# Moving weight splits of the second gate pair, the second up pair and the last gate matrix from POOL to DVE in a fused streaming-encoder block

## The chip, the cores and the metric

The kernel runs on one core of one Trainium2 chip. The metric is the device time of one execution in microseconds (us). Five queues of instructions run beside each other and meet at semaphores: TensorE (PE, with its weight loads as PEld), VectorE (DVE, `V` in the code), ScalarE (ACT, `A`), GpSimd (POOL, `G`) and SyncE (SP), which issues most transfers. Each engine takes its instructions strictly in the order of its queue.

## The reference

One layer over 1024 positions of 1024 features, all in float32. Cut to what matters here:

```python
u = rmsnorm(h, g_mix_pre);  z = u @ w_in            # ... gate_a, gate_b are two of its pieces
mixed = sigmoid(gate_a) * ya + sigmoid(gate_b) * yb # ya: conv mixer, yb: latent attention
h = h + rmsnorm(mixed @ w_o, g_mix_post)
u2 = rmsnorm(h, g_ffn_pre)
up = causal_dwconv3(u2 @ w_ffn_up) + b              # 2 x 2816 columns
f = (gelu(up[:, :2816]) * up[:, 2816:]) @ w_ffn_down
h = h + rmsnorm(f, g_ffn_post)
e = p @ w_ple_proj
g = sigmoid(h @ w_ple_gate)
return h + rmsnorm(e * g, g_ple_post)
```

## The kernel before, in words

**Three products for one.** Each operand of a matmul is held as a high part `hi` (the value cast to fp32r, L182, always on ACT) and a low part `lo` (value minus `hi`, L183, on the engine that the caller names). A product is hi·hi + lo·hi + hi·lo. `split` makes the two parts; `block` splits 512 columns, `wide` 1024 columns at once.

**Pairs.** The large products (`w_in`'s gates, `w_up`, `w_down`) are done by a scheme of seven instead of eight block products. For two 128-column blocks of weights, `weights` loads two 128x1024 tiles and forms combinations: it splits A22, adds A21 to A22 in place (L337), subtracts to make S3 (L338), then makes S1 (here L339), S2's and S4's tile (L340) and splits both tiles with `wide`. Its argument `who` names the engine for the split of A11/A12, for the split of A22, for L337 and for L338; L339, L340 and the last two splits are always DVE's. `pair` then runs the block products (`prod`, L307) into PSUM banks taken from a ring, and adds them up from PSUM on DVE (L367, L368, L377 to L383). An "early" pair has its first row done beforehand by `first_row`, and runs five products; its first sum, L366, is POOL's. The activations have the same kind of combinations (T1 to T4), made once a stage by `x_blocks`; `third` splits T3, T1 and T4.

**Three stages matter here.** In the gate stage (from about 70 us), pairs 2 to 5 of `w_in` come first; the first one's weights are made by DVE alone (`(V, V, V, V)`), those of the others by `(V, G, G, G)`. In the up stage (from about 815 us) the pairs follow `order`; again the first one's weights are DVE's, those of the rest are POOL's in the same four places. In the end stage (from about 1350 us) come the last products of the down projection (`down_tail`, L217, added up at L964), the norm of the second half of the features (`second_residual`, whose scaled rows are L1048, residual sums L1049 and splits the operand `hX`), then the gate product of the per-layer embedding with its own norm. `square_sum` squares on ACT (L250) and adds on DVE (L253).

**What sets the order.** The order within each queue is set when the kernel is built, by a scheduler that simulates the program; `tc.issue_after(x)` tells it only to place what is inside behind `x`, and adds no wait on the chip. Waits come from data, from PSUM banks and from the buffers ("slots", `s`) that are used again. `raws` is a ring of buffers for raw weights, `wblk` one of seven buffers for split weights.

Of the kernel before, what the change touches and what calls it, by code (L numbers as in the profile page):

```python
# [77 lines left out]
def kernel(  # L78
# [53 lines left out]
    def f32r(i):  # L132
        return slot(i, F32R)
# [7 lines left out]
    def singles(*slots):  # L141

        return [(i, h) for i in slots for h in range(2)]
# [5 lines left out]
    def f(ap):  # L149
        return ap.bitcast(F32)  # L150
# [39 lines left out]
        split(src, hi[:, :n], lo[:, :n], eng or G)  # L190
        return hi, lo

    def wide(src, eng):

        hi, lo = f32r(wblk()), f32r(wblk())
        split(src, hi, lo, eng)
        return [(hi[:, hs(i)], lo[:, hs(i)]) for i in range(2)]

    def load_w(src, raws, cols=1024, dst=(None, None), eng=None):

        raw = f32(raws())
        nc.sync.dma_start(raw[:, :cols], src)
        return [block(raw[:, c : min(c + HALF, cols)], eng, d) for c, d in zip(range(0, cols, HALF), dst)]

    def load_all(w, raws, others):

        where = [None] * NBLK + list(others)
        return [load_w(w[c], raws, dst=where[2 * c : 2 * c + 2]) for c in range(8)]

    def linear(out_ps, w, wc, X, half, cs=None, start=True, stop=True):  # L210

# [115 lines left out]
    def weights(src0, src1, raws, early=False, who=(V, G, G, G)):  # L327

        r0, r1 = f32(raws()), f32(raws())
        nc.sync.dma_start(r1, src1)  # L330
        nc.sync.dma_start(r0, src0)
        a11, a12, a21, a22 = r0[:, hs(0)], r0[:, hs(1)], r1[:, hs(0)], r1[:, hs(1)]
        w = {}
        if not early:
            w["A11"], w["A12"] = wide(r0, who[0])
        w["A22"] = block(a22, who[1])
        who[2].tensor_add(a22, a21, a22)  # L337
        w["S3 made"] = who[3].tensor_sub(a21, a11, a21)  # L338
        V.tensor_sub(a11, a22, a11)  # L339
        V.tensor_sub(a12, a12, a11)  # L340
        w["S2"], w["S4"] = wide(r0, V)
        w["S3"], w["S1"] = wide(r1, V)
        w["end"] = last[-1]
        return w
# [107 lines left out]
    def gate_weights(i, early=False, who=(V, G, G, G)):  # L452
        return weights(w_in[17 + 2 * i], w_in[18 + 2 * i], raws, early, who)
# [23 lines left out]
    for n, i in enumerate(range(2, 6)):  # L477
        if n:
            with tc.issue_after(behind):
                w = gate_weights(i, True)  # L480
        gate_pair(i, early[n], others(), True, w=w)
    for i in range(2):
        spilled_pair(i, early[i])
# [421 lines left out]
    mm = Ring(range(4))  # L905

    def up_weights(j):
        return weights(w_up[j], w_up[NFF + j], raws, j in rows, (G, G, G, G) if j != order[0] else (V, V, V, V))

    w = up_weights(order[0])  # L910
    behind = third(w)
# [119 lines left out]


    hrs = Ring(singles(12, 9))
    sqs, sqs2, accs = Ring(singles(extra[2])), Ring(singles(extra[3])), Ring(singles(50))
    hX = [[None, None] for _ in range(8)]
    hslots = [*range(29, 33), *range(13, 17)], range(17, 25)
    SS, RB = 6, 7

    def second_residual(h):
        acc = None  # L1040
        for k in range(8):
            acc = square_sum(acc, single(yacc[k], h), accs, sqs)
        R = rstd(acc, D, SS, RB)
        for k in range(8):
            hr = single(*hrs())
            nc.sync.dma_start(hr, d_h1[k, :, hs(h)])
            y = single(yacc[k], h)
            V.scalar_tensor_tensor(y, y, col("g_ffn_post", k), R, op0=ALU.mult, op1=ALU.mult)  # L1048
            (G if k % 2 else V).tensor_add(hr, hr, y)  # L1049
            hX[k][h] = parts(hslots[h][k])  # L1050
            split(hr, *hX[k][h], V if k % 2 else G)

    second_residual(0)
    down_tail(fX, 1)
    second_residual(1)

    mm = Ring(range(4))
    sbk, rbk = Ring([4, 5, 6]), Ring([7])
    ers, ors = Ring(singles(10, 11)), Ring(singles(42, 12, 9, 7, 8))
    wgs = load_all(w_gate, raws, [*range(25, 29), 43, *range(38, 42)])  # L1060
    for h, o, n in ((0, 0, 512), (1, 0, 256), (1, 256, 256)):
        acc = None
        cs = slice(o, o + n)
        base = h * HALF + o
        for ft in range(8):
            er = single(*ers())[:, :n]
            nc.sync.dma_start(er, d_e[ft, :, base : base + n])
            pt = bank(mm())[:, :n]
            linear(pt, wgs[ft], 0, hX, h, cs)
            g_ = single(yacc[ft], h)[:, cs]  # L1070
            A.activation(g_, pt, AF.Sigmoid)
            V.tensor_mul(g_, g_, er)  # L1072
            acc = square_sum(acc, g_, accs, sqs2)
        R = rstd(acc, D, sbk(), rbk(), n)
        for k in range(8):
            o_ = single(*ors())[:, :n]
            g_ = single(yacc[k], h)[:, cs]
            hi, lo = hX[k][h]
            G.tensor_add(o_, f(hi[:, cs]), f(lo[:, cs]))
            V.scalar_tensor_tensor(g_, g_, col("g_ple_post", k), R, op0=ALU.mult, op1=ALU.mult)  # L1080
            (G if k in (0, 2, 4) else V).tensor_add(o_, o_, g_)  # L1081
            (nc.sync if k % 2 else A).dma_start(out[k * P : (k + 1) * P, base : base + n], o_)
# [101 lines left out]
```

## Time and profile before

| | us |
|---|---|
| runs | 1517.89, 1518.36, 1521.10 |
| median | 1518.36 |
| profiled execution | 1521.76 |
| its span, first to last instruction | 1520.0 |

| engine | busy us | share of span | instructions |
|---|---|---|---|
| PE | 1472.8 | 97% | 6980 |
| PEld | 1227.8 | 81% | 6980 |
| DVE | 1180.4 | 78% | 1654 |
| ACT | 700.8 | 46% | 1100 |
| POOL | 522.7 | 34% | 383 |

PE works 97% of the span, so it stands for 47 us; the mean granted clock of this execution is 0.989 of full speed. The busy shares of the other engines are means over stages that differ much, and are read by stage below. All rows further down come from the profiled execution.

### The profile page before, as it was taken

The page shows a single profiled execution, that of the slowest core. Times are in us where ns is not written, and L with a number is a line of the kernel's source. Part 1 is how long each engine was busy: PE and PEld are TensorE (multiplying, and loading weights), DVE is VectorE, ACT ScalarE, POOL GpSimd, SP SyncE. Part 2 cuts the span into 40 slices and gives each one's busy share as a digit, 9 for nine tenths or more (in the row PEclk, how much of TensorE's full clock was granted, in tenths as well). Part 3 has the DMA queues.
Part 4 walks back from the last instruction along what each step waited for, and adds up shares of the span by engine and source line. Part 5 has one row for each costly group of instructions (what it writes and reads, how often), then busy time and mean ns, then how long its engine had stood idle before and what let it go on. Part 6 is the DMA issues. An engine that isn't in the chain of part 4 may idle for free. (4 is left out here: it accounts for less than half of the span.)

```text
span 1520.0 us, 19261 instructions
## 1 busy us (share of the span) xinstructions
PE 1472.8 (97%) x6980; PEld 1227.8 (81%) x6980; DVE 1180.4 (78%) x1654; ACT 700.8 (46%) x1100; POOL 522.7 (34%) x383
## 2 busy tenths in 40 slices
PE   8999999999989999999999999999999999999896
PEld 6878888888778888788887788888888888787796
DVE  6897666567558888753668889999998889978786
ACT  8634322336447777343454444444434634334333
POOL 1245122236533433341124243344331021333953
PEclk9999999999999999999999999999999999999898
DMA  9444322345841012542381223333335542433432
GB/s 343 158 140 157 122 78 59 114 171 187 272 165 48 20 56 88 190 140 63 118 300 45 97 89 119 125 125 114 114 120 175 183 168 70 125 118 111 140 105 96
DMA packets 74368, 198.72 MB, mean 131 GB/s; under 512 B 7456, under 2 KB 22304, under 8 KB 74272
## 3 DMA queue, kind: packets, MB, share of 16 engines
q1 hardware_dynamic: 65920, 173.04, 35.0%
q10 hardware_dynamic: 8352, 24.44, 4.2%
q8 instruction: 55, 0.90, 0.3%
q14 instruction: 41, 0.34, 0.1%
HBM read 144.89 MB, written 52.56 MB: 130 GB/s over the span
## 5 line engine op out<-in xcount | busy, mean ns | idle before, releaser
L307 PE MATMUL psum<-s,s 128*128 128x512 f32 x3948 | 906.5, 391 | 10.5 <-DVE s L367 5.2
L307 PEld LDWEIGHTS psum<-s,s 128*128 128x128 f32 x3948 | 742.7, 189 | 168.9 <-DVE s L367 5.6
L182 ACT CAST s<-s 128x1024 fp32r<-128x1024 f32 (+3 forms) x419 | 336.8, 828 | 400.6 <-PE psum L307 128.9
L217 PE MATMUL psum<-s,s 128*128 128x512 f32 (+1 forms) x1920 | 417.2, 375 | 17.3 <-ACT s L182 11.2
L183 POOL TENSOR_TENSOR s<-s,s 128x512 fp32r<-128x512 f32 (+2 forms) x147 | 219.9, 1508 | 558.5 <-PE psum L307 337.2
L217 PEld LDWEIGHTS psum<-s,s 128*128 128x128 f32 x1920 | 337.3, 192 | 81.3 <-ACT s L182 13.0
L183 DVE TENSOR_TENSOR s<-s,s 128x1024 fp32r<-128x1024 f32 (+2 forms) x272 | 325.3, 1215 | 65.0 <-ACT s L182 51.8
L543 DVE SCALAR_TENSOR_TENSOR psum<-s,vecs,psum 128x1023 f32<-128x1023 f32 (+1 forms) x88 | 111.7, 1278 | 4.3 <-ACT psum L541 3.3
L541 ACT ACTIVATE psum<-s,vecs 128x1024 f32<-128x1024 f32 x44 | 53.1, 1208 | 88.5 <-DVE s L379 74.3
L183 DVE TENSOR_TENSOR s<-psum,s 128x512 fp32r<-128x512 f32 (+3 forms) x144 | 70.8, 504 | 29.0 <-ACT s L182 27.9
L366 POOL TENSOR_TENSOR s<-s 128x512 f32<-128x512 f32 x24 | 45.8, 1908 | 135.5 <-DVE s L323 80.5
L182 ACT CAST s<-psum 128x512 fp32r<-128x512 f32 (+3 forms) x144 | 61.1, 445 | 41.8 <-DVE s L183 12.7
L250 ACT ACTIVATE s<-s 128x512 f32<-128x512 f32 (+1 forms) x68 | 38.9, 580 | 72.0 <-DVE s L1072 29.5
L762 PE MATMUL psum<-s,s 128*128 128x512 f32 (+2 forms) x288 | 67.4, 359 | 2.3 <-ACT s L773 2.2
L775 POOL TENSOR_SCALAR s<-s,ri 128x384 f32<-128x384 f32 (+5 forms) x48 | 41.3, 860 | 70.3 <-DVE ri L774 55.5
L253 DVE TENSOR_TENSOR s<-s,s 128x512 f32<-128x512 f32 (+1 forms) x55 | 46.3, 842 | 15.3 <-ACT s L250 13.6
L787 PE MATMUL psum<-s,s 128*128 128x256 f32 x320 | 54.1, 292 | 1.5 <-DVE s L183 0.7
L762 PEld LDWEIGHTS psum<-s,s 128*128 128x128 f32 x288 | 46.4, 189 | 9.9 <-ACT s L773 5.3
L773 ACT ACTIVATE s<-psum,nm 128x128 f32<-128x128 f32 (+3 forms) x64 | 47.5, 745 | 14.3 <-DVE nm L771 9.0
L338 POOL TENSOR_TENSOR s<-s,s 128x512 f32<-128x512 f32 x37 | 52.8, 1428 | 2.9
L337 POOL TENSOR_TENSOR s<-s 128x512 f32<-128x512 f32 x37 | 51.0, 1378 | 2.9
L253 DVE TENSOR_TENSOR s<-s,psum 128x512 f32<-128x512 f32 x28 | 19.1, 685 | 41.1 <-ACT psum L250 40.4
(120 smaller groups left out, 1180.4 us busy)
## 6 DMA issues: line engine op xcount, KB each, us to landing
s<-in_w_up_dram SPq DMA_DIRECT2D x56, 512.0 KB, 3.7
s<-in_w_in_dram SPq DMA_DIRECT2D x42, 512.0 KB, 3.9
s<-in_w_down_dram SPq DMA_DIRECT2D x36, 512.0 KB, 3.7
d_f<-s SPq DMA_DIRECT2D x22, 512.0 KB, 2.6
s<-in_x_dram SPq DMA_DIRECT2D x32, 256.0 KB, 5.4
d_sg<-s ACTq DMA_DIRECT2D x16, 512.0 KB, 2.9
s<-d_sg SPq DMA_DIRECT2D x16, 512.0 KB, 4.0
s<-d_f SPq DMA_DIRECT2D x16, 512.0 KB, 7.3
```

What stands on the lines that cost most here:

```text
L182: A.copy(hi, src)
L183: last.append((eng or V).tensor_sub(lo, src, f(hi)))
L217: nc.tensor.matmul(out_ps, w[c // HALF][pw][:, c % HALF : c % HALF + P], X[k][half][px][:, cs], start=start and a == 0 and k == 0, stop=st ...
L253: V.tensor_add(acc, acc, sq)
L307: nc.tensor.matmul(pt, w[pw][:, k * P : (k + 1) * P], blk[k][px], start=a == 0 and k == 0, stop=a == 2 and k == 3,)
L337: who[2].tensor_add(a22, a21, a22)
L338: w["S3 made"] = who[3].tensor_sub(a21, a11, a21)
L541: A.activation(dst, src, AF.Identity, bias=bias, scale=w2)
L543: V.scalar_tensor_tensor(dst[:, i:], src[:, : S - i], w, dst[:, i:], op0=ALU.mult, op1=ALU.add)
L762: nc.tensor.matmul(st_[:, lo_ : lo_ + w_], q[part_q][:, o : o + P], parts(K[hd, kh])[part_k][:, 0:w_], start=part_q == 0 and part_k == 0, ...
L773: A.activation(pr[:, 0:n], st_[:, 0:n], AF.Exp, bias=nm, accum_out=sm)
L787: nc.tensor.matmul(po[:, 0:256], vt[:, kt, :], t_[:, kk * 256 : (kk + 1) * 256], start=kt == 0 and part == 0, stop=kt == 2 * b + 1 and par ...
```

## The change

Three edits. First, the weights of the second early gate pair (`n == 1`) and of the second up pair (`order[1]`) get `(V, V, V, V)`: their A22 split, L337 and L338 go from POOL to DVE. Second, in the end stage the gate matrix is split by `wide_all`, as 8 splits of 128x1024 on DVE with 8 casts of that width on ACT, in place of 16 splits of 128x512 on POOL and 16 casts. Third, the squares of the last norms lie in PSUM banks instead of SBUF slots (banks 6 and 7 for the down norm, 4 and 5 for the last norm), and POOL's output sums `hi + lo` (L1079, now L1092) are to be placed behind the split of the seventh row of the same half.

```diff
@@ -190,9 +190,9 @@
         split(src, hi[:, :n], lo[:, :n], eng or G)
         return hi, lo
 
-    def wide(src, eng):
-
-        hi, lo = f32r(wblk()), f32r(wblk())
+    def wide(src, eng, at=(None, None)):
+
+        hi, lo = (f32r(wblk() if i is None else i) for i in at)
         split(src, hi, lo, eng)
         return [(hi[:, hs(i)], lo[:, hs(i)]) for i in range(2)]
 
@@ -206,6 +206,15 @@
 
         where = [None] * NBLK + list(others)
         return [load_w(w[c], raws, dst=where[2 * c : 2 * c + 2]) for c in range(8)]
+
+    def wide_all(w, raws, others):
+
+        where, ws = [None] * NBLK + list(others), []
+        for c in range(8):
+            raw = f32(raws())
+            nc.sync.dma_start(raw, w[c])
+            ws.append(wide(raw, V, where[2 * c : 2 * c + 2]))
+        return ws
 
     def linear(out_ps, w, wc, X, half, cs=None, start=True, stop=True):
 
@@ -477,7 +486,7 @@
     for n, i in enumerate(range(2, 6)):
         if n:
             with tc.issue_after(behind):
-                w = gate_weights(i, True)
+                w = gate_weights(i, True, (V, V, V, V) if n == 1 else (V, G, G, G))
         gate_pair(i, early[n], others(), True, w=w)
     for i in range(2):
         spilled_pair(i, early[i])
@@ -905,7 +914,7 @@
     mm = Ring(range(4))
 
     def up_weights(j):
-        return weights(w_up[j], w_up[NFF + j], raws, j in rows, (G, G, G, G) if j != order[0] else (V, V, V, V))
+        return weights(w_up[j], w_up[NFF + j], raws, j in rows, (V, V, V, V) if j in order[:2] else (G, G, G, G))
 
     w = up_weights(order[0])
     behind = third(w)
@@ -1031,8 +1040,9 @@
 
 
     hrs = Ring(singles(12, 9))
-    sqs, sqs2, accs = Ring(singles(extra[2])), Ring(singles(extra[3])), Ring(singles(50))
+    sqs, accs = Ring([6, 7]), Ring(singles(50))
     hX = [[None, None] for _ in range(8)]
+    h_ends = {}
     hslots = [*range(29, 33), *range(13, 17)], range(17, 25)
     SS, RB = 6, 7
 
@@ -1048,16 +1058,18 @@
             V.scalar_tensor_tensor(y, y, col("g_ffn_post", k), R, op0=ALU.mult, op1=ALU.mult)
             (G if k % 2 else V).tensor_add(hr, hr, y)
             hX[k][h] = parts(hslots[h][k])
-            split(hr, *hX[k][h], V if k % 2 else G)
+            end = split(hr, *hX[k][h], V if k % 2 else G)
+            if k == 6:
+                h_ends[h] = end.ins
 
     second_residual(0)
     down_tail(fX, 1)
     second_residual(1)
 
-    mm = Ring(range(4))
-    sbk, rbk = Ring([4, 5, 6]), Ring([7])
+    mm, sqs = Ring(range(4)), Ring([4, 5])
+    sbk, rbk = Ring([6]), Ring([7])
     ers, ors = Ring(singles(10, 11)), Ring(singles(42, 12, 9, 7, 8))
-    wgs = load_all(w_gate, raws, [*range(25, 29), 43, *range(38, 42)])
+    wgs = wide_all(w_gate, raws, [*range(25, 29), 43, *range(38, 42)])
     for h, o, n in ((0, 0, 512), (1, 0, 256), (1, 256, 256)):
         acc = None
         cs = slice(o, o + n)
@@ -1070,13 +1082,14 @@
             g_ = single(yacc[ft], h)[:, cs]
             A.activation(g_, pt, AF.Sigmoid)
             V.tensor_mul(g_, g_, er)
-            acc = square_sum(acc, g_, accs, sqs2)
+            acc = square_sum(acc, g_, accs, sqs)
         R = rstd(acc, D, sbk(), rbk(), n)
         for k in range(8):
             o_ = single(*ors())[:, :n]
             g_ = single(yacc[k], h)[:, cs]
             hi, lo = hX[k][h]
-            G.tensor_add(o_, f(hi[:, cs]), f(lo[:, cs]))
+            with tc.issue_after(h_ends[h]):
+                G.tensor_add(o_, f(hi[:, cs]), f(lo[:, cs]))
             V.scalar_tensor_tensor(g_, g_, col("g_ple_post", k), R, op0=ALU.mult, op1=ALU.mult)
             (G if k in (0, 2, 4) else V).tensor_add(o_, o_, g_)
             (nc.sync if k % 2 else A).dma_start(out[k * P : (k + 1) * P, base : base + n], o_)
```

Lines from L262 of the new kernel are those of before plus 9 (L253 is L262, L337 to L340 are L346 to L349, L367 is L376, L964 is L973), and after `second_residual` plus 10 to 13 (L1048 and L1049 are L1058 and L1059, L1072 is L1084, L1079 is L1092).

DVE at the second gate pair, before: `s38_634` is T4, `s42_90` and `s43_91` are the second pair's raw weight tiles, `s7_88` and `s34_102` belong to the first pair and to the rotary tables.

```order
L340 TENSOR_TENSOR s7_88<-s7_88 128x512
L183 TENSOR_TENSOR s38_634<-s34_102,s38_634 128x2x512 x2
L339 TENSOR_TENSOR s42_90<-s43_91,s42_90 128x512
L183 TENSOR_TENSOR s33_357<-s7_88,s3_137 128x1024
L340 TENSOR_TENSOR s42_90<-s42_90 128x512
L496 CAST s34_102<-s34_102 128x128
L497 TENSOR_SCALAR s34_102<-s34_102,vecs_70 128x128
L499 CAST ah_1363<-s34_102 128x128
```

Now:

```order
L349 TENSOR_TENSOR s7_88<-s7_88 128x512
L183 TENSOR_TENSOR s38_634<-s34_102,s38_634 128x2x512 x2
L183 TENSOR_TENSOR s5_391<-s43_91,s5_391 128x512
L183 TENSOR_TENSOR s33_357<-s7_88,s3_137 128x1024
L346 TENSOR_TENSOR s43_91<-s43_91 128x512
L505 CAST s34_102<-s34_102 128x128
L347 TENSOR_TENSOR s43_91<-s42_90,s43_91 128x512
L506 TENSOR_SCALAR s34_102<-s34_102,vecs_70 128x128
L348 TENSOR_TENSOR s42_90<-s43_91,s42_90 128x512
L508 CAST ah_1363<-s34_102 128x128
L349 TENSOR_TENSOR s42_90<-s42_90 128x512
```

The split of A22 (into `s5_391`), L346 and L347 stand between the last T4 split and L348; on POOL they are gone.

DVE at the second up pair, before: `s38_6246` is T4, `s7_88` and `s8_89` are the second pair's raw tiles, `s48_5010` and `s49_5011` the first pair's outputs.

```order
L183 TENSOR_TENSOR s38_6246<-s34_102,s38_6246 128x2x512 x2
L339 TENSOR_TENSOR s7_88<-s8_89,s7_88 128x512
L340 TENSOR_TENSOR s7_88<-s7_88 128x512
L183 TENSOR_TENSOR s3_137<-s7_88,s2_134 128x1024
L367 TENSOR_TENSOR s48_5010<-psum_69,s48_5010 128x512
L368 TENSOR_TENSOR s49_5011<-psum_69,s48_5010 128x512
L377 TENSOR_TENSOR s49_5011<-s49_5011,psum_69 128x512
L378 TENSOR_TENSOR s48_5010<-s48_5010,psum_69 128x512
L183 TENSOR_TENSOR s5_4893<-s8_89,s4_390 128x1024
L379 TENSOR_TENSOR s49_5011<-s49_5011,psum_69 128x512
```

Now:

```order
L183 TENSOR_TENSOR s38_6246<-s34_102,s38_6246 128x2x512 x2
L183 TENSOR_TENSOR s1_127<-s8_89,s1_127 128x512
L346 TENSOR_TENSOR s8_89<-s8_89 128x512
L347 TENSOR_TENSOR s8_89<-s7_88,s8_89 128x512
L348 TENSOR_TENSOR s7_88<-s8_89,s7_88 128x512
L376 TENSOR_TENSOR s48_5010<-psum_69,s48_5010 128x512
L349 TENSOR_TENSOR s7_88<-s7_88 128x512
L377 TENSOR_TENSOR s49_5011<-psum_69,s48_5010 128x512
L386 TENSOR_TENSOR s49_5011<-s49_5011,psum_69 128x512
L387 TENSOR_TENSOR s48_5010<-s48_5010,psum_69 128x512
L183 TENSOR_TENSOR s3_137<-s7_88,s2_134 128x1024
L183 TENSOR_TENSOR s5_4893<-s8_89,s4_390 128x1024
```

The three operations stand behind T4's splits, and the first pair's sums L376 to L387 (L367 to L378 before) now come ahead of both wide splits of the second pair, where before L367 stood behind the first of them.

DVE where the down products end, before: L964 adds a product of the last part into a row of the output, `s50_8660` is the sum of squares, `s49_9637` a square in SBUF, `s9_9132` a residual row, `s13_188` and `s29_8815` the operand `hX` of the first half.

```order
L964 TENSOR_TENSOR s48_5010<-s48_5010,psum_69 128x512
L183 TENSOR_TENSOR s29_8815<-s9_9132,s29_8815 128x512
L964 TENSOR_TENSOR s44_4934<-s44_4934,psum_69 128x512
L964 TENSOR_TENSOR s34_102<-s34_102,psum_69 128x512
L253 TENSOR_TENSOR s50_8660<-s50_8660,s49_9637 128x512
L1049 TENSOR_TENSOR s9_9132<-s9_9132,s44_4934 128x512
L253 TENSOR_TENSOR s50_8660<-s50_8660,s49_9637 128x512 x2
L1049 TENSOR_TENSOR s9_9132<-s9_9132,s48_5010 128x512
L964 TENSOR_TENSOR s46_4974<-s46_4974,psum_69 128x512
L253 TENSOR_TENSOR s50_8660<-s50_8660,s49_9637 128x512
L183 TENSOR_TENSOR s13_188<-s9_9132,s13_188 128x512
```

Now, down to the last such sum of the half (the first one, of `s48_5010`, stands just ahead):

```order
L262 TENSOR_TENSOR s50_8660<-s50_8660,psum_69 128x512
L183 TENSOR_TENSOR s25_624<-s8_89,s5_4893 128x1024
L973 TENSOR_TENSOR s46_4974<-s46_4974,psum_69 128x512
L262 TENSOR_TENSOR s50_8660<-s50_8660,psum_69 128x512
L973 TENSOR_TENSOR s44_4934<-s44_4934,psum_69 128x512
L1059 TENSOR_TENSOR s9_9132<-s9_9132,s44_4934 128x512
L183 TENSOR_TENSOR s13_188<-s9_9132,s13_188 128x512
L1059 TENSOR_TENSOR s9_9132<-s9_9132,s48_5010 128x512
L262 TENSOR_TENSOR s50_8660<-s50_8660,psum_69 128x512
L183 TENSOR_TENSOR s4_390<-s7_88,s3_137 128x1024
L183 TENSOR_TENSOR s13_188<-s9_9132,s13_188 128x512
L973 TENSOR_TENSOR s34_102<-s34_102,psum_69 128x512
```

The sums of squares read a bank; two of the eight wide splits of the gate matrix (`s25_624`, `s4_390`) and both low parts in `s13_188` now stand ahead of the last L973. The other six wide splits follow within the next nine rows.

## Rows read from the trace of the kernel before

**Rows 1.** Windows: us, length, busy (count) of PE, PEld, DVE, ACT, POOL, PEclk, DMA.

```profile
80.00:100.00 20.00, 18.27 (x72) 14.00 (x71) 19.26 (x31) 8.76 (x12) 6.89 (x5) 0.91 0.27 83
820.00:840.00 20.00, 14.31 (x59) 10.90 (x58) 13.44 (x13) 4.51 (x5) 14.32 (x7) 0.95 0.21 56
840.00:860.00 20.00, 20.00 (x80) 16.25 (x79) 16.37 (x19) 9.34 (x9) 7.87 (x5) 0.88 0.20 72
860.00:880.00 20.00, 20.00 (x90) 16.57 (x89) 18.18 (x20) 8.52 (x9) 5.38 (x4) 1.00 0.39 127
1400.00:1420.00 20.00, 15.85 (x55) 12.16 (x54) 17.36 (x19) 7.98 (x15) 19.46 (x13) 0.79 0.38 118
1420.00:1440.00 20.00, 20.00 (x88) 16.44 (x87) 13.89 (x14) 9.70 (x16) 20.00 (x15) 0.96 0.43 145
```

**Rows 2.** Timeline of PE: start, us, line, count, idle time before, releaser.

```profile
84.83 0.73 PE L307 MATMUL psum<-s,s 128*128 128x512 f32 x2 [1.11 <-DVE s L183]
838.81 7.43 PE L307 MATMUL psum<-s,s 128*128 128x512 f32 x19 [5.18 <-DVE s L367]
1372.99 6.42 PE L217 MATMUL psum<-s,s 128*128 128x512 f32 x27 [1.14 <-DVE s L183]
1411.55 2.50 PE L217 MATMUL psum<-s,s 128*128 128x512 f32 x5 [4.01 <-DVE s L964]
```

**Rows 3.** Timelines of POOL, DVE and ACT at the second gate pair.

```profile
75.16 1.83 POOL L183 TENSOR_TENSOR s<-s,s 128x512 fp32r<-128x512 f32 x1 [5.06 <-ACT s L182]
77.07 2.15 POOL L337 TENSOR_TENSOR s<-s 128x512 f32<-128x512 f32 x1
74.62 10.16 DVE L183 TENSOR_TENSOR s<-s,s 128x1024 fp32r<-128x1024 f32 x5
84.70 0.68 DVE L340 TENSOR_TENSOR s<-s 128x512 f32<-128x512 f32 x1
85.95 2.36 DVE L183 TENSOR_TENSOR s<-s,s 128x1024 fp32r<-128x1024 f32 x2 [0.57 <-ACT s L182]
81.48 1.05 ACT L182 CAST s<-s 128x1024 fp32r<-128x1024 f32 x1 [4.80 <-POOL s L338]
```

**Rows 4.** Timelines of POOL, ACT and DVE at the second up pair.

```profile
816.45 8.85 POOL L183 TENSOR_TENSOR s<-s,s 128x512 fp32r<-128x512 f32 x1 [35.12 <-PE psum L307]
825.38 1.29 POOL L337 TENSOR_TENSOR s<-s 128x512 f32<-128x512 f32 x1
828.07 3.46 ACT L182 CAST s<-s 128x1024 fp32r<-128x1024 f32 x4 [8.49 <-POOL s L338]
817.26 6.89 DVE L183 TENSOR_TENSOR s<-s,s 128x1024 fp32r<-128x1024 f32 x6
830.10 2.36 DVE L183 TENSOR_TENSOR s<-s,s 128x1024 fp32r<-128x1024 f32 x2 [5.35 <-ACT s L182]
838.08 0.68 DVE L367 TENSOR_TENSOR s<-psum,s 128x512 f32<-128x512 f32 x1
```

**Rows 5.** Timelines of DVE, POOL and PE in the end stage.

```profile
1405.79 3.44 DVE L253 TENSOR_TENSOR s<-s,s 128x512 f32<-128x512 f32 x2
1409.16 1.74 DVE L1049 TENSOR_TENSOR s<-s,s 128x512 f32<-128x512 f32 x1
1410.82 0.67 DVE L964 TENSOR_TENSOR s<-s,psum 128x512 f32<-128x512 f32 x1
1414.91 14.71 POOL L183 TENSOR_TENSOR s<-s,s 128x512 fp32r<-128x512 f32 x11
1454.79 1.74 POOL L183 TENSOR_TENSOR s<-s,s 128x512 fp32r<-128x512 f32 x1
1459.73 4.00 PE L217 MATMUL psum<-s,s 128*128 128x256 f32 x32
```

**Rows 6.** The page, costliest groups: DVE sums of squares, from SBUF and PSUM.

```profile
L253 DVE TENSOR_TENSOR s<-s,s 128x512 f32<-128x512 f32 (+1 forms) x55 | 46.3, 842 | 15.3 <-ACT s L250 13.6
L253 DVE TENSOR_TENSOR s<-s,psum 128x512 f32<-128x512 f32 x28 | 19.1, 685 | 41.1 <-ACT psum L250 40.4
```

## The prediction

> **What bounds the kernel now.** I read the page first: PE is busy for 97% of the span, so a change that leaves its matmuls alone can only win where PE stands or runs slowly. The timeline of PE gives the places, and windows of 20 us show what each costs. An undisturbed window holds 90 matmuls at a granted clock of 1.00, which is 20 / 90 = 0.222 us each [rows 1]. Three places fall short, and the change has a part at each.
>
> Gate stage, 80 to 100 us: PE idles 20 - 18.27 = 1.73 us, and a mean clock of 0.91 costs 0.09 x 20 = 1.8 us: 3.5 us (18 matmuls fewer than 90 would be 4.0). The largest stall, 1.11 us, ends with a DVE split [rows 1, 2].
>
> Up stage, 820 to 860 us: idle 20 - 14.31 = 5.69, clock 0.95 and 0.88, which is 1.0 + 2.4: 9.1 us. The count agrees: 31 + 10 matmuls missing, 41 x 0.222 = 9.1. One stall of 5.18 us, ended by DVE's L367, is most of it, and the clock falls to its 1.2 GHz level behind it [rows 1, 2].
>
> End stage: 1.14 us before 1372.99; in 1400 to 1440 us idle 4.15 and clock 0.79 and 0.96, which is 4.2 + 0.8. Sum 10.3 us. The stall of 4.01 us is ended by DVE's L964 [rows 1, 2].
>
> Together 3.5 + 9.1 + 10.3 = 22.9 us. That is the most these places hold.
>
> **Part 1, the second gate pair.** It takes three operations from POOL and adds them to DVE. On POOL the split and the addition took 1.83 and 2.15 us, and the ACT cast that waited 4.80 us for the third ran at 81.48. Beside them DVE's five splits took 10.16 us, 2.03 each; two such splits with POOL silent took 2.36, 1.18 each [rows 3]. So POOL's departure gives 10.16 - 5 x 1.18 = 4.3 us back to DVE before 84.78, and the last split, for which PE came at 84.83 - 1.11 = 83.72, ends near 80.5. The three new operations cost DVE 3 x 0.68 = 2.0 us (a 512-column operation with both inputs in SBUF, POOL silent), behind the T4 splits [rows 3]. The stall goes and so does the reason for the slow clock: 3.5 us at most. DVE is busy 19.26 of 20 us there [rows 1], so the 2.0 us may come out again at a later pair. I take -3.2; bounds -4.0 (by the count) and +2.0, where DVE hands its whole new work on to PE.
>
> **Part 2, the second up pair.** The chain of before: POOL's A22 split began at 816.45 and lasted 8.85 us, while DVE did its six splits; the addition began at 825.38 and took 1.29 us. ACT waited 8.49 us for the last of the three, until 828.07; DVE waited 5.35 us for ACT, until 830.10; and L367, queued behind that pair's first wide split, ran at 838.08 and freed PE's bank [rows 4]. Now the three stand on DVE behind T4's splits: free at 817.26 + 6.89 + 0.68 (one sum from PSUM beside the splits) = 824.8, so done by 824.8 + 3 x 0.68 = 826.8. L376 and the sums after it stand ahead of the wide splits, as the order above shows; L376 needs only L348 to have passed, about 827.5, and PE came for the bank at 838.81 - 5.18 = 833.6. That is 6 us of room, so the stall, and the slow clock behind it, should go: 9.1 us. What is late next is the second pair's own wide splits, queued behind L387, which waits for a product of PE's; two more products (24 matmuls, 5.3 us) then cover two splits (2.4 us) and their casts. DVE carries 18.18 of 20 us in the windows that follow [rows 1], so a little may come back. I take -8.8; bounds -9.5 and +2.0 (the stall stays DVE's and the new 2.0 us are added to it).
>
> **Part 3, the end stage.** Taken from DVE: sums of squares read PSUM, 685 ns instead of 842 in the mean [rows 6], and where POOL was busy more: two took 3.44 us just ahead of the late L964, and an L1049 took 1.74 [rows 5]. In the stretch between the sums L964, three of these become 3 x 0.685, some 3 us less, and L1059 may fall to 0.68, 1.1 less, where POOL rests. Added to DVE: eight wide splits of 1.18 us at least, 9.4 us in all, 2.4 of them ahead of the last L973, and two low parts of `hX` at 0.68. So the late sum comes 4.1 - 2.4 - 0.7 = 1.0 us earlier on its own chain, and the earlier sums of the norm, 6 or 7 of them now 0.685, give some 1 to 2 us more. The stall of 4.01 shrinks to about 2, in pieces. Whether the clock falls behind it I give an even chance: half of 5.0 us. The 1.14 us before 1372.99 waited for a split queued behind SBUF sums of squares and mostly goes (1.0); the eleven POOL splits of 14.71 us that stood ahead of the residual sums of the second half [rows 5] are gone, which moves that half's operand earlier. It was ready at 1454.79 + 1.74 = 1456.5, and PE first used it at 1459.73 [rows 5]: some 3 us in hand, and PE will come 6 us sooner, so this gain is needed. ACT is busy at most 9.70 of 20 us there [rows 1], so its casts, 8 of 1024 columns for 16 of 512, hide. POOL's output sums behind its splits cost nothing where nothing waits for them. Sum 1.0 + 2.0 + 2.5 + 0.5 (for smaller stalls of the last norm) = 6.0. Bounds: -10.3, all of it, and +8.5, from the third rival.
>
> Row and rule: with POOL busy a split of 1024 columns took 2.03 us and alone 1.18 [rows 3], and in [rows 5] sums with two SBUF inputs took 1.72 while the L964 beside them, with one input in PSUM, took 0.67. The Trainium skill ("SBUF — State Buffer", Who interferes with whom) says that an operation of DVE with two SBUF inputs contends with reads of GpSimd, and one with a single SBUF input does not; the trace agrees. By that rule the third edit cuts both ways: the sums of squares escape POOL, but the wide splits don't, and by it the two ahead of the last L973 would take 2 x 0.85 = 1.7 us more, and part 3 would give 4.3 instead of 6.0.
>
> **Sum.** 3.2 + 8.8 + 6.0 = 18.0 us from the profiled execution's 1521.76 gives 1503.8. That execution is 3.4 us above the median of 1518.36, so the median after should be 1500.4 us. Whether a change can be told from none is a matter of 0.2% here, 3 us.
>
> **Rivals.**
> First, the end stage gains nothing: DVE's eight splits meet POOL's sums and take 2.03 each, a new stall takes the place of the 4.01, and the slow clock stays. For it: DVE is already busy 17.36 of 20 us in that window [rows 1]. Against it: most of POOL's 19.46 us there are gone. Time: 1500.4 + 6.0 = 1506.4.
> Second, the up stage gives its gain back: DVE, at 18.18 of 20 us for the rest of the stage [rows 1], gets 2.0 us more, and stays late. For it: the stall's releaser was DVE's L367. Against it: DVE had itself waited 5.35 us for a chain that began on POOL [rows 4]. Losing 7 of the 8.8: 1507.4.
> Third, slower: DVE is the bound at all three places, and its own backlog, not POOL, decides. Then the gate stall stays and 2.0 us are added, likewise at the up stage, and in the end stage eight splits at 2.03, 16.2 us, less 16 x 0.157 = 2.5 us from the squares, put 13.7 us on DVE's chain; with 5.1 us of slow clock PE loses 18.8 instead of 10.3, 8.5 more. Time: 1518.4 + 2.0 + 2.0 + 8.5 = 1530.9. It decides only if DVE's idle time of 20 - 13.44 us in the up window [rows 1] and of 2.6 to 6.1 us a window in the end stage can't take the added work; the waits on ACT and POOL in [rows 4] speak against it.
> Fourth, the places are cleared wholly: 22.9 instead of 18.0, 1495.5.
>
> **Chances.** Forecast 0.55, first rival 0.18, second 0.11, fourth 0.07, first and second together (about 1513) 0.05, third 0.04. The forecast's own range is 1496.5 to 1504. For 8 in 10 I add the fourth and most of the first two: 1495 to 1508. Faster by over 0.2% is all but the third rival and some of the double one: 0.92; within 0.2%: 0.04; slower: 0.04.
>
> **What would show it.** In the changed kernel's trace: no PE stall ended by a DVE split between 80 and 100 us, and a clock of 1.00 there; DVE's T splits at 1.2 us instead of 2.03. In the up stage no stall at L376, clock 1.00 in both windows, no wait of ACT for POOL before the second pair. In the end stage sums of squares near 0.68 us each, POOL's busy share between 1400 and 1440 us well under 19 of 20, PE's stall at L973 under 3 us. The prediction is wrong if a PE stall of over 4 us ended by DVE stands anywhere in these stretches, or if new stalls between 860 and 1160 us show DVE as the releaser.

## The result, and the profile after

The changed kernel takes 1497.85 us (median of four runs, 1496.04 to 1499.31) against 1518.12 us for the kernel before in the same comparison (1516.32 to 1521.10): 20.3 us less, ratio 0.9861, interval [0.9842, 0.9880]. (Here and below the ratio is an estimate over all runs of a comparison, and can differ a little from that of the two medians.) Measured once more beside the last experiments, it took 1498.70 against 1516.93, 18.2 us less. The prediction was 1500.4 us, 18.0 less, with a range of 1495 to 1508. The profiled execution took 1496.72 us, its span 1494.9 us; PE is busy 1461.2 us of it, granted clock 0.996.

Windows of the changed kernel (columns as in [rows 1]); its up stage runs some 6 us earlier than before and its end stage 15 to 25 us earlier, so the stretches are not the same to the microsecond:

```profile
80.00:100.00 20.00, 20.00 (x90) 16.57 (x89) 19.39 (x37) 8.66 (x11) 5.20 (x4) 1.00 0.32 110
820.00:840.00 20.00, 20.00 (x89) 16.33 (x88) 19.18 (x21) 6.23 (x7) 9.83 (x6) 1.00 0.19 61
840.00:860.00 20.00, 20.00 (x90) 16.55 (x89) 18.75 (x23) 10.70 (x11) 6.35 (x6) 1.00 0.38 132
1380.00:1400.00 20.00, 19.87 (x87) 15.95 (x86) 19.39 (x20) 9.52 (x15) 14.75 (x8) 1.00 0.74 227
1400.00:1420.00 20.00, 20.00 (x96) 16.67 (x95) 14.72 (x27) 12.68 (x18) 6.14 (x4) 1.00 0.32 113
1420.00:1440.00 20.00, 19.06 (x109) 16.47 (x107) 14.49 (x19) 7.97 (x15) 16.25 (x12) 1.00 0.25 79
```

The three places of [rows 1] are full, with a clock of 1.00: PE is busy 20.00 us in the first two, where there were 18.27 at 0.91 and 14.31 at 0.95, and 19.87 us in 1380 to 1400, in which now falls what stood in 1400 to 1420 before (15.85 at 0.79). The next two fences are the timelines behind that; first DVE and ACT at the second gate pair and the second up pair, which answer to [rows 3, 4]:

```profile
75.48 5.76 DVE L183 TENSOR_TENSOR s<-s,s 128x1024 fp32r<-128x1024 f32 x5
810.77 6.90 DVE L183 TENSOR_TENSOR s<-s,s 128x1024 fp32r<-128x1024 f32 x6
818.18 3.46 DVE L183 TENSOR_TENSOR s<-s,s 128x1024 fp32r<-128x1024 f32 x3
825.81 0.68 DVE L376 TENSOR_TENSOR s<-psum,s 128x512 f32<-128x512 f32 x1
824.21 1.05 ACT L182 CAST s<-s 128x1024 fp32r<-128x1024 f32 x1 [4.11 <-DVE s L347]
```

The five T splits take 5.76 us (1.15 each) instead of 10.16, with POOL silent. At the up pair L376 ran at 825.81, behind four operations of the second pair's weights (its A22 split and L346 to L348), but ahead of their wide splits; ACT waits 4.11 us, for DVE's own L347, and nothing of PE's hangs on it. In the end stage, DVE and PE, answering to [rows 5]:

```profile
1388.83 0.67 DVE L262 TENSOR_TENSOR s<-s,psum 128x512 f32<-128x512 f32 x1
1392.27 0.67 DVE L973 TENSOR_TENSOR s<-s,psum 128x512 f32<-128x512 f32 x1
1392.87 3.96 DVE L183 TENSOR_TENSOR s<-s,s 128x1024 fp32r<-128x1024 f32 x2
1370.62 34.15 PE L226 MATMUL psum<-s,s 128*128 128x512 f32 x147
```

One sum of squares (L262, of 128x512) takes 0.67, the last L973 runs at 1392.27, and PE goes through 147 matmuls without a stall that shows. Of the sums of squares in [rows 6], 63 instead of 28 now read PSUM; 20 of the 55 others, outside the last two norms, still read SBUF. (In the 63 are some of 256 columns, which pull the mean down.)

```profile
L262 DVE TENSOR_TENSOR s<-s,psum 128x512 f32<-128x512 f32 (+1 forms) x63 | 39.3, 625 | 46.7 <-ACT psum L259 44.5
L262 DVE TENSOR_TENSOR s<-s,s 128x512 f32<-128x512 f32 x20 | 15.6, 779 | 6.5 <-ACT s L259 5.7
```

**Where the time came from.** The starts of the same matmuls in both traces cut the span into five stretches. The cuts are the matmuls at 374.81, 617.78, 1247.94, 1317.83 and 1510.92 us of the trace before; in that of the changed kernel they are at 370.30, 611.86, 1232.82, 1302.96 and 1486.17. The last column is what the same stretch took in those experiments below whose kernels don't touch it.

| stretch (has) | before | changed | difference | untouched elsewhere |
|---|---|---|---|---|
| start to 374.81 (part 1) | 374.8 | 370.3 | -4.5 | 373.5 to 375.0 |
| to 617.78 (attention's inputs, attention) | 243.0 | 241.6 | -1.4 | 241.6 to 245.0 |
| to 1247.94 (part 2) | 630.2 | 621.0 | -9.2 | 627.4 to 628.0 |
| to 1317.83 | 69.9 | 70.1 | +0.2 | 69.8 to 70.3 |
| to 1510.92 (part 3) | 193.1 | 183.2 | -9.9 | 192.5 to 193.0 |

The profiled execution of before was a costly one in its up stage: 2.4 us over what five other kernels with the same code there took. Against the means of those kernels the parts give 374.2 - 370.3 = 3.9, 627.8 - 621.0 = 6.8 and 192.8 - 183.2 = 9.6, together 20.3 us, beside the 20.3 and 18.2 of the medians. That it agrees so well with the first is in part chance: each stretch is from one execution of a kernel, and the second, which no part of the change touches, moves by 3.4 us from kernel to kernel.

### The profile page after: what moved, and what is told of

Read it like the earlier page. It is cut to its first block, busy times and chain, and to the rows that moved or that the text cites. A ratio compares the mean times of both kernels' runs of the same rounds, so it can differ in the third digit from the quotient of the medians.

```text
span 1494.9 us, 19240 instructions
## 1 busy us (share of the span) xinstructions
PE 1461.2 (98%) x6980; PEld 1220.6 (82%) x6980; DVE 1162.5 (78%) x1668; ACT 702.8 (47%) x1094; POOL 505.1 (34%) x361
## 5 line engine op out<-in xcount | busy, mean ns | idle before, releaser
L316 PEld LDWEIGHTS psum<-s,s 128*128 128x128 f32 x3948 | 739.9, 188 | 158.5 <-ACT s L182 2.6
L226 PE MATMUL psum<-s,s 128*128 128x512 f32 (+1 forms) x1920 | 412.1, 372 | 10.1 <-ACT s L182 8.9
L226 PEld LDWEIGHTS psum<-s,s 128*128 128x128 f32 x1920 | 333.7, 190 | 73.1 <-ACT s L182 11.6
L183 DVE TENSOR_TENSOR s<-s,s 128x1024 fp32r<-128x1024 f32 (+2 forms) x282 | 329.6, 1190 | 58.4 <-ACT s L182 44.7
L183 POOL TENSOR_TENSOR s<-s,s 128x512 fp32r<-128x512 f32 (+2 forms) x129 | 189.6, 1482 | 491.9 <-PE psum L316 289.8
L375 POOL TENSOR_TENSOR s<-s 128x512 f32<-128x512 f32 x24 | 68.3, 2844 | 158.6 <-DVE s L332 80.4
L262 DVE TENSOR_TENSOR s<-s,psum 128x512 f32<-128x512 f32 (+1 forms) x63 | 39.3, 625 | 46.7 <-ACT psum L259 44.5
L348 DVE TENSOR_TENSOR s<-s,s 128x512 f32<-128x512 f32 x45 | 45.8, 1017 | 12.2 <-POOL s L347 12.0
L771 PEld LDWEIGHTS psum<-s,s 128*128 128x128 f32 x288 | 46.4, 189 | 9.9 <-ACT s L782 5.3
L347 POOL TENSOR_TENSOR s<-s,s 128x512 f32<-128x512 f32 x35 | 49.7, 1419 | 2.7
L796 PEld LDWEIGHTS psum<-s,s 128*128 128x128 f32 x320 | 45.4, 189 | 6.1 <-DVE s L183 2.0
L386 DVE TENSOR_TENSOR s<-s,psum 128x512 f32<-128x512 f32 x47 | 32.1, 682 | 21.2 <-PE psum L316 21.2
```

Of the source, the lines that this page charges most:

```text
L183: last.append((eng or V).tensor_sub(lo, src, f(hi)))
L226: nc.tensor.matmul(out_ps, w[c // HALF][pw][:, c % HALF : c % HALF + P], X[k][half][px][:, cs], start=start and a == 0 and k == 0, stop=st ...
L316: nc.tensor.matmul(pt, w[pw][:, k * P : (k + 1) * P], blk[k][px], start=a == 0 and k == 0, stop=a == 2 and k == 3,)
L375: G.tensor_add(d11, d11, m1)
L771: nc.tensor.matmul(st_[:, lo_ : lo_ + w_], q[part_q][:, o : o + P], parts(K[hd, kh])[part_k][:, 0:w_], start=part_q == 0 and part_k == 0, ...
L796: nc.tensor.matmul(po[:, 0:256], vt[:, kt, :], t_[:, kk * 256 : (kk + 1) * 256], start=kt == 0 and part == 0, stop=kt == 2 * b + 1 and par ...
```

## The experiments

**Each part alone.** The edits are the three hunks of the diff, taken singly:

```diff
 e1_gate: +  w = gate_weights(i, True, (V, V, V, V) if n == 1 else (V, G, G, G))
 e2_up:   +  (V, V, V, V) if j in order[:2] else (G, G, G, G)
 e3_end:  +  wide_all, sqs in PSUM, issue_after(h_ends[h])
```

> Only part 1: the kernel before with the second gate pair's A22 split, addition and S3 on VectorE. My theory (POOL's chain and its contention with VectorE's T splits make the stall): no TensorE stall between 80 and 100 us, clock 1.00 there, splits of 1024 columns at 1.2 us instead of 2.03, 3 to 4 us less, about 1514.5; the up and end stages keep their stalls of about 5 and 4 us. Rival (VectorE is full there, and hands its 2.0 us of new work on): a stall of 1 us or more at a later gate pair, 0 to 2 us more.

> Only part 2: the second up pair's three operations on VectorE. My theory: the stall of 5.18 us at the product that waits for L367 and the slow clock behind it go, 8.8 to 9.2 us less, about 1509. Rival (VectorE, over 90% busy in the stage, hands it back): a new stall released by VectorE between 840 and 1160 us, 0 to 3 us less.

> Only part 3: wide splits of the gate matrix on VectorE, the last norms' squares in PSUM, POOL's output sums behind its splits. Theory after the result: the stalls of 1.14 and 4.01 us and the slow clock behind go altogether, 10 us less, about 1508. Rival, as I had it in the prediction: a stall of some 2 us stays in pieces and the clock falls in half of the executions, 6 us less. Gate and up stage keep their stalls of 1.7 and 5.7 us in sum.

Measured: part 1 1513.94 us, ratio 0.9977 [0.9965, 0.9989]; part 2 1512.07, 0.9956 [0.9940, 0.9972]; part 3 1508.08, 0.9931 [0.9914, 0.9947], beside 1517.29 for the kernel before. By their ratios the three fall by 0.23, 0.44 and 0.69%, which adds up to 1.36%; the whole change gave 1.39%. By the medians it is 3.4, 5.2 and 9.2 us, 17.8 in sum, against 20.3 and 18.2. So the parts add up, as far as runs that vary by some us can show. Parts 1 and 3 gave what was expected, part 2 less than its 8.8 to 9.2 us. The rivals of each fall: the timelines show no PE stall of 0.5 us or more in part 1's stretch after the start, none at all between 800 and 1200 in part 2's, and in part 3's nothing over 0.3 us until the last norm. Part 2's trace also shows the two stages that it leaves alone, PE's timeline and a window:

```profile
84.42 0.73 PE L307 MATMUL psum<-s,s 128*128 128x512 f32 x2 [1.11 <-DVE s L183]
1401.64 2.50 PE L217 MATMUL psum<-s,s 128*128 128x512 f32 x5 [4.00 <-DVE s L964]
```

```profile
80.00:100.00 20.00, 18.26 (x78) 14.21 (x77) 19.26 (x28) 8.01 (x10) 8.43 (x6) 1.00 0.28 83
```

The stalls of [rows 2] are there unchanged, 1.11 and 4.00 us. But the window at the gate pair has a clock of 1.00 with the same idle time, 20 - 18.26 = 1.74 us, where the kernel before had 0.91: the same stall is followed by the slow clock in one execution and not in another. Of the seven profiled executions that have this stall, three had the slow clock behind it (before, e5_psum and e7_order) and four had not. Yet the first stretch took 374.8 us in the mean of the three and 373.9 in that of the four: in the four PE lost more at its next stall, near 127 us, that a DVE split of the third pair ends.

**Part 3 in pieces.** One of its three edits at a time:

```diff
 e4_wide: +  wgs = wide_all(w_gate, ...)
 e5_psum: +  sqs, accs = Ring([6, 7]), ...     +  mm, sqs = Ring(range(4)), Ring([4, 5])
 e6_sums: +  with tc.issue_after(h_ends[h]):  G.tensor_add(o_, ...)
```

> Of part 3 only the wide splits of the gate matrix on VectorE (squares stay in SBUF, POOL's output sums where they were). Theory: POOL's share of the time between 1380 and 1440 us falls from 20 of 20 to 6 to 16, so VectorE's sums with two SBUF inputs run in 0.7 us again; most of the end stage's gain comes from here, 6 to 9 us less, about 1510. Rival (the squares in PSUM carry it, the wide splits cost VectorE 9.4 us): no gain or a new stall ended by VectorE, 0 to 3 us more.

> Of part 3 only the squares of the last norms in PSUM. Theory: sums of squares fall to 0.68 us, some 3 us come off VectorE between the sums L964, the stall of 1.14 us goes and that of 4.01 becomes 1 to 2; 2 to 5 us less, about 1514. Rival (the squares in PSUM carry all of part 3): both stalls and the slow clock go, 9 to 10 us less, about 1508.

> Of part 3 only POOL's output sums placed behind its splits. Both theories: two sums of 1.3 to 1.7 us leave POOL between 1402 and 1409 us, its splits come earlier by as much, the stall at L964 (4.01 us) stays within 1 us; 0 to 1.5 us less, about 1517.

Measured: 1516.94 us, ratio 0.9989 [0.9977, 1.0001]; 1515.45, 0.9973 [0.9961, 0.9985]; 1519.27, 0.9999 [0.9985, 1.0013], beside 1518.65. The wide splits alone, window and PE's timeline:

```profile
1400.00:1420.00 20.00, 16.97 (x63) 13.34 (x62) 20.00 (x16) 9.88 (x13) 11.78 (x7) 0.83 0.53 164
```

```profile
1407.38 14.33 PE L226 MATMUL psum<-s,s 128*128 128x512 f32 x49 [3.03 <-DVE s L973]
```

POOL falls from 19.46 to 11.78 of 20 us, but DVE is now busy all 20.00, and PE still stalls 3.03 us for DVE's L973, with the slow clock behind (0.83). The squares in PSUM alone:

```profile
1400.00:1420.00 20.00, 15.82 (x73) 12.02 (x72) 15.06 (x23) 9.21 (x18) 19.95 (x16) 1.00 0.50 154
```

```profile
1403.88 0.73 PE L217 MATMUL psum<-s,s 128*128 128x512 f32 x2 [1.27 <-ACT s L182]
1405.61 3.53 PE L217 MATMUL psum<-s,s 128*128 128x512 f32 x14 [0.99 <-DVE s L964]
1412.11 5.28 PE L217 MATMUL psum<-s,s 128*128 128x512 f32 x22 [1.81 <-ACT s L182]
```

DVE has room (15.06), POOL none (19.95), and three stalls stay, two of them behind casts that ACT makes late. The wide splits alone missed their theory of 6 to 9 us and came near its rival, with a stall that DVE ends. The squares alone gave 3.2 us by the medians, within their theory of 2 to 5.

How much each piece carries isn't settled. The stretch that ends at 1510.92 took 190.6 us with the wide splits, 186.9 with the squares in PSUM, 192.3 with the moved sums and 183.7 with all three: 2.2, 5.9 and 0.5 us off 192.8, in sum 8.6, and 9.1 together. But the profiled execution with the squares (1512.81 us, no slow clock at this place) is the second fastest of twelve. By the medians of the runs the pieces give 1.7, 3.2 and none, and all three 9.2; by the ratios 0.11, 0.27 and 0.01%, against 0.69. So by the runs the whole is more than its pieces, at the edge of what the intervals allow. The squares are the largest piece, and the moved sums alone give nothing that shows.

**What the pieces lack.** DVE is hardly freer with all three edits (19.39 of 20 us in 1380 to 1400) than with the wide splits alone (20.00), so its load doesn't explain why no stall is left. The order of PE's queue does, and neither the diff nor the working speaks of it: the scheduler places PE's matmuls of this stretch anew as well. The gate product that waits for the last sum L964 needs that sum's PSUM bank. Counted in the queues that the kernels build, and timed in the traces:

| | last sum ends behind the last down product | matmuls between | PE's stall for it |
|---|---|---|---|
| before | 7.8 us | 15 | 4.01 us |
| wide splits alone | 7.1 | 18 | 3.03 |
| squares alone | 5.6 | 14 | 0.99 |
| all three | 5.7 | 37 | none |

In the changed kernel the 16th matmul behind the last down product starts at 1390.87 and the last L973 ends at 1392.94: in its old place the waiting matmul would have stalled 2.1 us. In its new place it starts at 1395.99. So DVE's shorter way takes about half of the stall, and the 22 matmuls that now come first (22 x 0.222 = 4.9 us) cover the rest. No run changes this order by itself, so this is read from traces and queues and not tested.

**Contention or chain at the gate pair.** Work was given back to POOL without giving back the chain:

```diff
+            with tc.issue_after(sums[0]):      # sums[0]: the first pair's L375
+                for _ in range(6):
+                    G.tensor_add(single(46, 0), f(B["B22"][0][0]), f(B["B22"][0][1]))
 e12_memset, in place of these:   for _ in range(12):  G.memset(f32(46), 0.0)
```

> The changed kernel with six sums of 128x512 on POOL added where POOL had worked for the second gate pair before (they write a slot that nothing reads); nothing waits for them but POOL's own queue. If contention of POOL with VectorE's T splits made the stall of before: the five splits take about 2.0 us each again instead of 1.15, and TensorE idles 1 us or more near 84 us with a slow clock behind it, 2 to 4 us more than the changed kernel (about 1500.5). If the chain through POOL's S3 and the ACT cast behind it made the stall: splits are slower, TensorE doesn't stall, about 1498.

> The twin of the run with six added sums: the changed kernel with twelve memsets of 128x1024 on POOL in their place, which read no SBUF. If POOL's reads are what holds up VectorE's splits: the five T splits take 1.15 us each as in the changed kernel, no TensorE stall near 84 us, about 1498. If POOL's mere work does it: 1.6 to 2.0 us each and 3 us of stalls, about 1502.

Measured: 1503.80 us with the sums (two runs), 1500.81 with the memsets (two runs), the changed kernel 1498.70 beside the latter. With the sums, DVE's T splits and PE's stalls:

```profile
77.24 9.03 DVE L183 TENSOR_TENSOR s<-s,s 128x1024 fp32r<-128x1024 f32 x5
76.73 6.18 POOL L490 TENSOR_TENSOR s<-s 128x512 f32<-128x512 f32 x3
81.83 0.73 PE L316 MATMUL psum<-s,s 128*128 128x512 f32 x2 [1.03 <-DVE s L183]
84.05 4.14 PE L316 MATMUL psum<-s,s 128*128 128x512 f32 x16 [1.49 <-DVE s L183]
```

And with the memsets:

```profile
75.00 6.86 DVE L183 TENSOR_TENSOR s<-s,s 128x1024 fp32r<-128x1024 f32 x5
76.18 8.06 POOL L490 MEMSET s<- 128x1024 f32 x8
```

Five splits took 9.03 us beside POOL's sums and PE stalled 1.03 and 1.49 us for them, with no chain through POOL at all; beside memsets they took 6.86 us, and PE didn't stall. Split by split it is plainer. In the run with the sums three of the five began while POOL summed and took 2.30 or 2.31 us each, and two began when it had ended and took 1.21. In the run with the memsets the first ran beside a POOL sum (L375, until 76.24) and took 2.31, and the four beside memsets took 1.21. The matmul of 374.81 before came at 375.13 with the sums and at 371.06 with the memsets (370.43 in the changed kernel's second profile), so only 0.6 of the 2.1 us by which the memset run was slower lie here. So contention is enough to make a stall of this size, and POOL's reads make the contention. The sums are not the old work again: they began at 69.62 instead of 75.16 and slowed two earlier splits as well (4.32 us instead of 2.36), PE stalled at earlier matmuls, the cost was above the 2 to 4 us expected, and the slow clock that was expected didn't come (1.00 in 80 to 100 us). That contention made the stall of before as well follows from its own trace: there the five splits of 10.16 us follow each other without a gap, so none of them waited for the chain. The Trainium skill ("SBUF — State Buffer", Who interferes with whom) says that a DVE operation with two SBUF inputs contends with a GpSimd instruction that reads SBUF and not with one that only writes it: the two runs agree.

**Order or chain at the up pair.** POOL keeps its three operations; only L367 is placed ahead of DVE's work on the second pair's weights:

```diff
+        with tc.issue_after(late) if late else ExitStack():   # late: the first pair's L367
             V.tensor_sub(a11, a22, a11)
             V.tensor_sub(a12, a12, a11)
             w["S2"], w["S4"] = wide(r0, V)
```

> The kernel before with another order alone: the first up pair's sum L367 placed ahead of VectorE's work on the second pair's weights (L339, L340 and the wide splits); POOL keeps its three operations. If the stall of 5.18 us came from the place of L367 behind those: it ran at 838.08 and would run at about 832.4, behind the T4 splits that ACT casts late; the stall of 5.18 goes, another of 1 to 3 us may come where the second pair's S2 is late; 4 to 8 us less, about 1512. If the chain through POOL is itself on the path (ACT's T4 casts behind the cast that waits for POOL): a stall of 3 to 5 us stays, 0 to 3 us less.

Measured: 1515.32 us beside 1518.65, ratio 0.9970 [0.9956, 0.9985]. DVE, ACT and PE at the place (L368 is the old L367):

```profile
829.19 2.36 DVE L183 TENSOR_TENSOR s<-s,s 128x1024 fp32r<-128x1024 f32 x2 [5.36 <-ACT s L182]
831.47 0.68 DVE L368 TENSOR_TENSOR s<-psum,s 128x512 f32<-128x512 f32 x1
827.15 3.47 ACT L182 CAST s<-s 128x1024 fp32r<-128x1024 f32 x4 [8.39 <-POOL s L338]
830.15 5.30 PE L307 MATMUL psum<-s,s 128*128 128x512 f32 x22 [0.22 <-ACT s L182]
836.08 11.18 PE L307 MATMUL psum<-s,s 128*128 128x512 f32 x48 [0.62 <-ACT s L182]
848.54 1.66 PE L307 MATMUL psum<-s,s 128*128 128x512 f32 x6 [1.28 <-DVE s L368]
```

The chain is as late as before: ACT waits 8.39 us for POOL, DVE 5.36 us for ACT [rows 4: 8.49 and 5.35]. Yet L368 runs at 831.47 instead of 838.08, and of the stall of 5.18 us small ones of 0.22, 0.62 and 1.28 are left, the clock 1.00 in both windows. The stretch took 624.2 us, against 627.8 for untouched ones and 620.8 with part 2. So about half of part 2's gain is order alone, 3.6 of 7.0 us from one profile each, which lies between the two expectations. The other half comes only with POOL's three operations on DVE. That the late chain is what it takes away is argued from the casts that end two of the small stalls; it wasn't parted from POOL's reads beside DVE.

**A version that might be faster still.** In the changed kernel PE stalled 2.50 us at 397.55, behind four DVE low parts of the rotary key that took 6.22 us beside POOL's splits; a second edit goes for the stalls near 1300 us:

```diff
 e9_key:  +  split(kr[a : a + 64, hs(h)], hi[a : a + 64], lo[a : a + 64], G)
 e10_sq:  +  with tc.issue_after(ends[1]) if h == k == 0 else ExitStack():  acc = square_sum(...)
```

> The changed kernel again, beside the two that follow. About 1497.9, 20 us under the kernel before; in its profile no TensorE stall at the three places, a stall of about 2.5 us near 397 us and 2 to 3 us near 1300.

> The changed kernel, with the five low parts of the rotary key (64x512, two SBUF inputs) on POOL instead of VectorE. In the changed kernel four of them took 6.22 us on VectorE beside POOL's splits, and TensorE stalled 2.50 us behind them with a slow clock. If contention with POOL is what makes it: that stall and the slow clock go, 2 to 4.5 us less, about 1494.5. Rival (POOL comes late with the query splits that now stand behind): a stall released by POOL between 400 and 440 us, 0 to 3 us more.

> As the last, and the first square of the down norm placed behind the second down pair's weights, since ACT's casts stood behind that square, which waited 2.41 us for a sum on POOL. If so the stalls near 1300 us (1.09 + 0.70 + 0.35) shrink, 0.5 to 2 us less than the last, about 1493. Rival (the casts wait for VectorE and transfers anyway): no difference.

Measured: the changed kernel 1498.70 us (ratio 0.9886 [0.9870, 0.9903]), the key on POOL 1497.95 (0.9876 [0.9861, 0.9890]), both edits 1499.28 (0.9883 [0.9868, 0.9898]): no difference. PE of the run with the key on POOL, and of the one with both near 1300 us:

```profile
426.40 7.51 PE L226 MATMUL psum<-s,s 128*128 128x512 f32 x26 [3.83 <-ACT s L182]
1302.73 2.11 PE L316 MATMUL psum<-s,s 128*128 128x512 f32 x8 [0.69 <-ACT s L182]
```

The stall near 397 went and one of 3.83 us came at 426.40, for an ACT cast; in the changed kernel's two profiles the same matmul came at 427.28 and 426.62, with 0.37 and 2.29 us of stall. (In the second of them the stall near 397 was only 0.58 us, so it too was priced from one execution.) Whatever PE gains ahead of it, it waits there until about 427. The trace with the key on POOL shows what lies behind that cast, DVE and ACT:

```profile
424.94 1.42 DVE L633 SCALAR_TENSOR_TENSOR s<-s,vecs,s 128x512 f32<-128x512 f32 x2 [4.17 <-DMA s<-d_l]
425.73 1.28 ACT L182 CAST s<-s 128x512 fp32r<-128x512 f32 x2 [3.97 <-DVE s L633]
```

The cast waits for DVE's L633, and that for the load of a latent row (d_l), which is issued at 419.3 only. What an earlier load would give wasn't tried. The stalls near 1300 us stayed as they were, so that theory of mine is wrong.

## Why the prediction was right, and where its sizes were off

**Part 1**, -3.2: 3.6 us in its own run's stretch (374.2 - 370.6), 3.9 in the changed kernel's. Right, and for the reason given first, the 4.3 us that POOL's silence gives back to DVE. Half of the price was a slow clock that only three of seven executions have there; that the size holds all the same is due to the next stall, near 127 us, which the working didn't see and which goes too. That the 2.0 us of new work might come out again did not happen.

**Part 2**, -8.8: the stall and the slow clock went as worked out, and 9.2 us between the two profiles. The size was taken from one execution, and a costly one; other executions of the same code lose 6.8 to 7.0 us there. The working had both the new order and the shorter chain, but didn't tell them apart: the order alone is worth about half.

**Part 3**, -6.0: this term was mis-sized, 9.1 to 9.6 us measured. The step that failed is "The stall of 4.01 shrinks to about 2, in pieces", with the even chance for the slow clock that hangs on it (2.0 + 2.5). For DVE's side it was right: with PE's queue as it was, 2.1 us would have been left. But it took the place of the waiting matmul in PE's queue as fixed. It now stands behind 37 matmuls instead of 15, and neither the rest of the stall nor the slow clock is left. The fourth rival, in which the places are cleared wholly, is what came in this stretch.

The errors have opposite signs: part 2 was put 2.0 us too high, parts 1 and 3 some 0.7 and 3.6 too low. The 18.0 us were priced in an execution 3.4 us above the median and then taken off the median in full, so the surplus of 2.4 us in the up stage was counted though the median doesn't have it. That 18.0 forecast and 20.3 measured lie so near is partly luck.

The first rival (eight splits overload DVE) is what the wide splits do alone, with DVE at 20.00 of 20 us and a stall of 3.03. With the squares in PSUM DVE is as good as full too (19.39), but nothing of PE's waits for it. The second rival, the up stage handing its gain back, falls: DVE is busy 18.75 to 19.18 us in the two windows from 820 us, and PE loses nothing. The third falls with both. The rule on POOL's reads would have made part 3 give 4.3, by 1.7 us more in the two wide splits ahead of the last L973. These took 1.22 and 1.21 us; two behind it did take 3.96 beside POOL's output sums, but nothing waited for them.

## What to carry to other kernels

Moving an operation off an engine pays twice where its reads slow a neighbour's work, as POOL's did with DVE's splits (2.31 us beside them, 1.21 without): price the neighbour's slow-down with the chain. When an edit goes through a scheduler, compare the order of every queue, the one that waits too: here PE's own order took half of a stall away. And take a stall's price from several executions of the same code, since the slow clock behind it comes in some and not in others.

## What the runs showed of the hardware that was not expected

The slow clock (1.2 GHz) doesn't follow the idle time in sum. With the squares in PSUM alone PE idled 20 - 15.82 = 4.2 us in 1400 to 1420 us, in three pieces, and the clock stayed at 1.00; the kernel before idled 4.15 us in that window, nearly all in one piece, and had 0.79 [rows 1]. Whether the pieces make the difference isn't shown: that is one execution of each, and at the gate pair the same short stalls had the slow clock behind them in three of seven.

Contention can fall on POOL's side alone. One sum of 128x512 took 24.05 us in the changed kernel beside DVE's preparation of the up stage (24.32 in its second profile), where the next POOL operation of that size took 1.29. DVE's splits beside it were not slowed, six in 6.90 us, where at the gate pair DVE's were. The sum ended at 818.82, just behind DVE's first operation there with an input in PSUM (L372, 817.58 to 818.27). Spans on POOL are rough; the 8.85 us of the split in [rows 4], the same case in the kernel before, is borne out by the next operation, which began 8.93 us after it. What decides which side is held up isn't shown.

```profile
794.77 24.05 POOL L375 TENSOR_TENSOR s<-s 128x512 f32<-128x512 f32 x1 [20.09 <-ACT s L334]
822.35 1.29 POOL L183 TENSOR_TENSOR s<-s,s 128x512 fp32r<-128x512 f32 x1 [3.53 <-PE psum L316]
```
